# A recorded program, its list scheduler and pinned engine orders in a two-layer hybrid backbone

## The chip, the cores and the metric

One NeuronCore of a Trainium2 chip runs the whole program in one launch. The metric is the device time of an execution in microseconds (us). A difference counts as one only from about 1% on.

## The reference, cut to what matters

Two layers work on 512 latent tokens and 256 context tokens, 1024 wide, in fp32:

```python
for i in range(DEPTH):
    sh1_l, sc1_l, g1_l, sh2_l, sc2_l, g2_l = adaln(c, ada_w[i], ada_b[i])       # silu(c) @ w + b, six sections
    sh1_c, sc1_c, g1_c, sh2_c, sc2_c, g2_c = adaln(c_ctx, ada_w[i], ada_b[i])
    h_l = rmsnorm(x, norm1_g[i]) * (1.0 + sc1_l) + sh1_l
    h_c = rmsnorm(ctx, norm1_g[i]) * (1.0 + sc1_c) + sh1_c
    p_l, p_c = h_l @ w_in[i], h_c @ w_in[i]      # Hyena | gMLP gating | differential attention
    ...
    x = x + g1_l * mix_out(p_l, att_l, hy_params, sg_params, w_out[i])
    x = x + g2_l * swiglu(rmsnorm(x, norm2_g[i]) * (1.0 + sc2_l) + sh2_l, ffn_w1[i], ffn_w2[i])
    if not last:
        ...                                      # the same for ctx
```

The Hyena part convolves with long filters that a small sine MLP gives; they depend on weights alone.

## The kernel before

Each fp32 product is three matmuls of fp32r halves (`mm3`, L251 to L253: high by high, high by low, low by high). What feeds them is split into halves by `split`: ScalarE (ACT) copies the high half (L232) and VectorE (DVE) subtracts for the low half (L233); for weights the raw tile is FW and the halves lie in RW, for activations F and R. The matmuls write into eight PSUM banks (one tile, `banks`). SBUF is four arenas (F, FW, R, RW), and a buffer's place in them is fixed while the Python code runs, so a later buffer waits for the earlier one's readers.

Four generators are woven by rates that the code states: the latent stream, the context stream, a side task (filters and their spectra, from the long-convolution tables), and the modulation (`ada`). The weaving fixes the order in which instructions are recorded. The framework then takes, at the end of its context, each engine's order from these records and its own estimates of durations; an engine issues in the order that it was given.

The names that the prediction uses: `filters` multiplies position features by two small layers (matmuls at L859), and reduces and takes the sine on DVE and ACT (L863, L818 to L824); the result is stored at L870 as `hid`, and `spectra` reads it back (L885) and multiplies it at L905 and L906. `ada` (matmuls at L400) works in steps: a step loads two tiles of 512 KB (L364) and has eight matmuls of 32 columns by 256, four side by side in four column strips of the array; four steps make a section, and sections 0 and 1 give the first layer's modulation. FW holds six such tiles. `norm` squares on ACT and adds on DVE (L459), takes 1/sqrt by a chain of small DVE instructions (L261 to L267, L283), and scales (L482, L506, L507, L510). `attend` reduces a maximum (L686), scales it (L689), takes the exponential on ACT (L691), combines (L695 to L697) and transposes (L706). DMAs of x, ctx and weights are issued by SyncE (SP), the tables by GpSimd (POOL).

```python
for z in range(2):
    for j in range(4):
        k = 2 * i + z
        nc.tensor.matmul(pa[32 * j:32 * j + 32, :], lhsT=self.cv[:, k, :],
                         rhs=ws[j // 2][:, j % 2, z], start=(k == 0), stop=(k == KT - 1),
                         tile_position=(0, 32 * j))
```

Of the kernel before, what the change touches and what calls it, by code (L numbers as in the profile page):

```python
# [2 lines left out]

# [6 lines left out]
F32 = mybir.dt.float32  # L10
# [3 lines left out]
ALU = mybir.AluOpType  # L14
# [18 lines left out]
CW = 256  # L33
# [5 lines left out]
class Buf:  # L39


    def __init__(self, arena, pos, units, ap):
        self.arena, self.pos, self.units, self.ap = arena, pos, units, ap
# [69 lines left out]
class Stream:  # L113


    def __init__(self, name, T, v, home, away, mine):
# [18 lines left out]
POOL = {"in cm": (0, 1),  # L135
        "in tm": (0, 0),
        "out": (0, 1),
        "rope": (0, 0),
        "parity": (1, 0),
        "product 1": (1, 1),  # L140
        "product 2": (1, 0),
        "mix": (0, 2)}
# [7 lines left out]
class Net:  # L150
# [16 lines left out]
    def woven(self, *tasks):  # L167

        live = [[g, r, 0.0, False] for g, r in tasks]
        phase = self.phase
        while live:
            if self.phase != phase:
                phase = self.phase
                for t in live:
                    t[2] = 0.0
            t = min(live, key=lambda t: t[2])
            before = self.cost
            try:  # L180
                t[3] = next(t[0]) == "wait"
            except StopIteration:
                live.remove(t)
                continue
            t[2] += max(self.cost - before, 1.0) / (self.rates[t[1]] if isinstance(t[1], str) else t[1])
            yield "wait" if all(o[3] for o in live) else None
# [1153 lines left out]
def run(gen):  # L1340
    stuck = 0
    for r in gen:
        stuck = stuck + 1 if r == "wait" else 0
        assert stuck < 1000


def network(ctx, tc, A):
    net = Net(ctx, tc, A)
    woven = net.woven
    kd = {(l, L): tc.dram_tile([P, 2, 2, 2, L // 256, HYW], F32, name=f"kd{l}_{L}")  # L1350
# [124 lines left out]
    def side_task():  # L1475
        yield from fil
        yield from spectra(0, SEQ)
        yield from spectra(0, CTX)
        yield from wait("late")
        yield from spectra(1, SEQ)  # L1480
# [26 lines left out]
    side = side_task()  # L1507
    net.first = []
    gens = {"A": ada, "F": fil, "L": lat_gen, "C": con_gen, "S": side, **{k: loads(k) for k in "XBDK"}}
    for g, n in START:  # L1510
        run(take(gens[g], n))
    run(woven((lat_gen, "lat"), (con_gen, "con"), (side, "side"),
              (ada, "ada")))


def flat(ap):
# [106 lines left out]
```

## Time and profile before

| what | value |
|---|---|
| median of 3 runs | 1918.73 us (1917.03 to 1928.58) |
| the profiled execution | 1918.05 us |
| its span, first to last instruction | 1916.3 us |
| mean granted TensorE clock | 0.963 of 2.4 GHz |
| TensorE (PE) matmuls busy | 1797.2 us, 94% |
| VectorE (DVE) busy | 1079.3 us, 56% |
| ScalarE (ACT) busy | 676.9 us, 35% |

Matmuls are pipelined and their ends are modelled, so a duration of one matmul is longer than its distance to the next; distances are read from starts. The matmuls of L400 are recorded twice each, so a step of eight shows as x16.

### The profile page before, as it was taken

What the parts mean: (1) busy time and instruction counts of PE and PEld (TensorE: products, weight loads), DVE (VectorE), ACT (ScalarE), POOL (GpSimd) and SP (SyncE); (2) the same over time, 40 slices, a digit from 0 to 9 for tenths busy, and PEclk for the clock granted to TensorE, in tenths of its full rate; (3) what the DMA queues carried; (4) which work ended last, traced back from release to release, by engine and by line L of the source; (5) the groups of instructions that cost most, each with busy time, mean ns of one, the idle gap of its engine ahead of it and who ended that gap; (6) DMA issues with size and microseconds to landing.
All of it is one profiled execution on the core that took longest, in us unless ns stands there. A gap on an engine that the chain in (4) does not pass through costs nothing.

```text
span 1916.3 us, 27513 instructions
## 1 busy us (share of the span) xinstructions
PE 1797.2 (94%) x10938; PEld 1532.3 (80%) x10938; DVE 1079.3 (56%) x2243; ACT 676.9 (35%) x1167; POOL 118.0 (6%) x127
## 2 busy tenths in 40 slices
PE   4799898888997999999999999899999999999999
PEld 1478798677776888888888888789988798888887
DVE  5677786876868533332323244779588773333333
ACT  2534434443535321212121222633455452222221
POOL 1100223311001000000000000011000000000000
PEclk9799899799997999999999999899999899999999
DMA  8667644335454434343424135453213222323321
GB/s 274 198 222 237 212 155 133 111 101 162 144 174 137 153 99 136 90 136 110 149 86 146 61 112 174 138 171 124 72 43 111 73 62 64 115 83 102 93 93 65
DMA packets 101819, 245.39 MB, mean 128 GB/s; under 512 B 9748, under 2 KB 21750, under 8 KB 101690
## 3 DMA queue, kind: packets, MB, share of 16 engines
q1 hardware_dynamic: 93450, 221.71, 36.3%
q0 software_dynamic: 8240, 21.92, 3.9%
q8 instruction: 86, 1.41, 0.3%
q14 instruction: 43, 0.35, 0.1%
HBM read 221.18 MB, written 22.41 MB: 127 GB/s over the span
## 4 chain that ended last, share of the span: by engine, by line
PE 72%; DVE 7%; ACT 2%; issue 1%; DMA 1%; POOL 0%; DVEq 0%; ACTq 0%
PE banks L251 23%; PE banks L252 22%; PE banks L253 22%; PE banks L706 1%; PE banks L400 1%; DVE tiny L686 1%; PE banks L279 1%; DMA F<-x_ctx 1%; DVE F L459 1%; DVE RW L233 0%; ACT F L506 0%; ACT F L691 0%; DVE F L1028 0%; DVE F L1189 0%; DVE F L1026 0%
## 5 line engine op out<-in xcount | busy, mean ns | idle before, releaser
L251 PE MATMUL banks<-R,RW 128*128 128x512 f32 (+1 forms) x1984 | 698.3, 353 | 8.1 <-ACT R L507 2.9
L252 PE MATMUL banks<-R,RW 128*128 128x512 f32 (+1 forms) x1984 | 695.2, 351 | 2.6 <-DVE R L510 2.6
L253 PE MATMUL banks<-R,RW 128*128 128x512 f32 (+1 forms) x1984 | 693.4, 350 | 1.7 <-DVE RW L233 1.7
L232 ACT ACTIVATE RW<-FW 128x1024 fp32r<-128x1024 f32 (+2 forms) x240 | 240.3, 1002 | 563.9 <-PE banks L252 427.5
L251 PEld LDWEIGHTS banks<-R,RW 128*128 128x128 f32 x1984 | 379.0, 191 | 66.8 <-issue 5.6
L252 PEld LDWEIGHTS banks<-R,RW 128*128 128x128 f32 x1984 | 378.8, 191 | 51.9 <-DVE R L510 3.9
L253 PEld LDWEIGHTS banks<-R,RW 128*128 128x128 f32 x1984 | 378.1, 191 | 50.1 <-DVE RW L233 2.1
L233 DVE TENSOR_TENSOR RW<-FW,RW 128x1024 fp32r<-128x1024 f32 (+2 forms) x228 | 263.1, 1154 | 243.5 <-ACT RW L232 225.7
L1189 DVE SCALAR_TENSOR_TENSOR F<-banks,mods,F 128x512 f32<-128x512 f32 (+1 forms) x192 | 116.3, 615 | 177.1 <-PE banks L253 150.6
L251 PE MATMUL banks<-R 128*128 128x256 f32 (+3 forms) x584 | 185.0, 336 | 30.7 <-ACT R L1039 12.3
L252 PE MATMUL banks<-RW,R 128*128 128x256 f32 x624 | 178.9, 287 | 2.3 <-DVE RW L233 2.2
L251 PE MATMUL banks<-RW,R 128*128 128x256 f32 x624 | 180.1, 289 | 0.8 <-ACT RW L232 0.7
L253 PE MATMUL banks<-RW,R 128*128 128x256 f32 x624 | 179.0, 287 | 0.0
L252 PE MATMUL banks<-R 128*128 128x256 f32 (+3 forms) x584 | 176.6, 316 | 0.0
L253 PE MATMUL banks<-R 128*128 128x256 f32 (+3 forms) x584 | 175.2, 312 | 1.3 <-DVE R L1041 1.3
L251 PEld LDWEIGHTS banks<-R 128*128 128x128 f32 (+1 forms) x584 | 114.8, 205 | 55.9 <-ACT R L1039 14.6
L1207 DVE TENSOR_TENSOR F<-F,banks 128x256 f32<-128x256 f32 (+1 forms) x71 | 40.0, 565 | 203.8 <-PE banks L253 189.9
L232 ACT ACTIVATE R<-F 128x512 fp32r<-128x512 f32 (+1 forms) x133 | 71.8, 550 | 222.9 <-DVE F L1207 159.8
L252 PEld LDWEIGHTS banks<-R 128*128 128x128 f32 (+1 forms) x584 | 117.5, 205 | 8.8 <-issue 3.0
L252 PEld LDWEIGHTS banks<-RW,R 128*128 128x128 f32 x624 | 120.8, 194 | 4.6 <-DVE RW L233 3.7
L251 PEld LDWEIGHTS banks<-RW,R 128*128 128x128 f32 x624 | 120.8, 194 | 3.7 <-issue 1.0
L253 PEld LDWEIGHTS banks<-RW,R 128*128 128x128 f32 x624 | 120.9, 194 | 0.7 <-issue 0.2
(158 smaller groups left out, 1681.1 us busy)
## 6 DMA issues: line engine op xcount, KB each, us to landing
FW<-in_ffn_w SPq DMA_DIRECT2D x104, 512.0 KB, 3.7
FW<-in_ada_w SPq DMA_DIRECT2D x96, 512.0 KB, 5.3
FW<-in_w_in_tm SPq DMA_DIRECT2D x50, 512.0 KB, 4.7
R<-in_tab POOLq DMA_DIRECT2D x28, 512.0 KB, 5.9
FW<-in_w_in_cm SPq DMA_DIRECT2D x24, 512.0 KB, 4.7
F<-x_ctx SPq DMA_DIRECT2D x36, 256.0 KB, 3.4
FW<-in_ffn_w SPq DMA_DIRECT2D x24, 384.0 KB, 3.1
x_ctx<-F SPq DMA_DIRECT2D x32, 256.0 KB, 2.4
```

Of the source, the lines that this page charges most:

```text
L232: self.nc.scalar.activation(hi, src, AF.Copy)
L233: (lo_eng or self.nc.vector).tensor_tensor(lo, src, hi.bitcast(F32), op=ALU.subtract)
L251: mm(out, lhsT=lh, rhs=rh, start=(i == 0), stop=False)
L252: mm(out, lhsT=lh, rhs=rl, start=False, stop=False)
L253: mm(out, lhsT=ll, rhs=rh, start=False, stop=(i == n - 1))
L279: nc.tensor.matmul(p1[:, t:t + 1], lhsT=sq[:, t * P:(t + 1) * P], rhs=self.ones[:, 0:1], start=True, stop=True)
L400: nc.tensor.matmul(pa[32 * j:32 * j + 32, :], lhsT=self.cv[:, k, :], rhs=ws[j // 2][:, j % 2, z], start=(k == 0), stop=(k == KT - 1), tile ...
L459: nc.vector.tensor_tensor(st.acc[:, cols], st.acc[:, cols], q.ap, op=ALU.add)
L686: nc.vector.tensor_reduce(m, b.ap, axis=AX.X, op=ALU.max)
L706: nc.tensor.transpose(p[:, i, z, :], ws[z][:, (a + i) * P:(a + i + 1) * P], self.ident)
L1189: self.nc.vector.scalar_tensor_tensor(x, p, self.mods[l][:, sec * 8 + k, st.v:st.v + 1], x, op0=ALU.mult, op1=ALU.add)
L1207: nc.vector.tensor_tensor(s.ap, s.ap, u, op=ALU.mult)
```

## The change

The code that records instructions runs as before, but on `Plan`, which notes each call with a duration and a pace instead of issuing it. At the end `needs` finds who waits for whom from the regions that calls read and write, `order` runs a list scheduler, and `issue` issues all calls in its order and ties each instruction to the one before it on its engine, so that the framework can't move it. The scheduler takes, whenever an engine is free, the call that can start with the lowest rank: three quarters by its place in the recorded order, one quarter by the longest chain of work that still hangs on it. `note` joins the eight matmuls of an `ada` step into one entry. No computation, buffer or DMA is changed.

```diff
+class Plan:
...
+    RATE, LINE, HANDOVER, DRAIN, LANDING, WINDOW = 2.4, 258.0, 38.0, 163.0, 1620.0, 3413.0
+    def __init__(self, tc, share=0.75):
...
+    def note(self, e, op, args, kw):
...
+        if op == "dma_start":
+            took, pace = math.prod(out.shape) * 4 / self.LINE, 50.0 if e == self.SP else 560.0
+        elif e == self.PE:
+            if op == "transpose":
+                pace, late, ins = 109.0, [args[1]], [args[2]]
+            else:
+                lhs, rhs = kw["lhsT"], kw["rhs"]
+                n, late, ins = size(rhs), [lhs], [rhs]
+                if rhs.dtype != F32 or lhs.dtype != F32:
+                    pace = max(n / self.RATE + 13.5, 109.0)
+                elif size(lhs) <= 32:
+                    pace = 125.0
+                else:
+                    pace = 2 * max(112.0, n / self.RATE)
+            took = pace + self.DRAIN
...
+        elif e == self.POOL:
+            took = 340 + 2.1 * n if kw.get("op") != ALU.pow else 700 + 180 * n
+            pace = took - 40
+        else:
...
+            took = (n + {"tensor_tensor": 148, "tensor_scalar": 155}.get(op, 205 if op[0] == "s" and n > 64 else 140)) / 0.96
+            pace = took - 82
+        call, glue = (op, args, kw), e == self.PE and n == CW and size(out) == CW and size(late[0]) == 32
+        units = [[u for x in side for u in self.region(x)] for side in (outs, ins, late)]
+        if glue and self.todo and self.todo[-1][2]:
+            last = self.todo[-1]
+            last[1].append(call)
...
+    def order(self):
+        todo, needs = self.todo, self.needs()
+        n = len(todo)
+        rest, behind = [0.0] * n, [[] for _ in todo]
+        for k in range(n - 1, -1, -1):
+            rest[k] += todo[k][3] + (self.LANDING if todo[k][1][0][0] == "dma_start" else 0.0)
+            for j, kind in needs[k].items():
+                rest[j] = max(rest[j], rest[k])
+                behind[j].append((k, kind))
+        top = max(rest)
+        rank = [self.share * k / n - (1 - self.share) * rest[k] / top for k in range(n)]
...
+    def issue(self):
+
+        nosync = mybir.DependencyInfo(mybir.DependencyClass.NoSync, mybir.DependencyReason.DATA)
+        last = [None] * 5
+        for k in self.order():
+            e, calls = self.todo[k][:2]
+            for op, args, kw in calls:
+                ins = getattr(getattr(self.tc.nc, Program.engines[e]), op)(*args, **kw).ins
+                if last[e] is not None:
+                    self.tc.add_manual_dep(ins, last[e], nosync, reason="order")
+                last[e] = ins.name
...
 def network(ctx, tc, A):
+    tc = Plan(tc)
     net = Net(ctx, tc, A)
...
     run(woven((lat_gen, "lat"), (con_gen, "con"), (side, "side"),
               (ada, "ada")))
+    tc.issue()
```

Every instruction of the changed kernel carries the line of the call in `issue` (L1571), so its rows are told apart by their tiles.

The first place is the program's head, on SP, whose queue issues the loads of x, the modulation weights (`in_ada_w`), ctx, and the store of the MLP's result (`hid`). Before:

```order
L421 DMA F<-in_x 128x1024 x4
L364 DMA FW<-in_ada_w 128x2x512 x5
L421 DMA F<-in_ctx 128x512 x4
L364 DMA FW<-in_ada_w 128x2x512 x7
L870 DMA hid<-F 128x768
L885 DMA F<-in_hy_w 64x1024 x2
L885 DMA F<-hid 64x512 x2
L894 DMA F<-in_decay 128x1024
L896 DMA F<-in_hy_bias 1x512
L364 DMA FW<-in_ada_w 128x2x512 x4
```

And now:

```order
L1571 DMA FW<-in_ada_w 128x2x512
L1571 DMA F<-in_x 128x1024
L1571 DMA FW<-in_ada_w 128x2x512 x5
L1571 DMA subs_83<-in_subln_g 128x2
L1571 DMA F<-in_ctx 128x512 x3
L1571 DMA F<-in_hy_w 64x1024 x2
L1571 DMA F<-in_ctx 128x512
L1571 DMA F<-in_decay 128x1024
L1571 DMA hid<-F 128x768
L1571 DMA FW<-in_ada_w 128x2x512 x8
L1571 DMA F<-in_hy_bias 1x512
L1571 DMA F<-hid 64x512 x2
```

Six modulation tiles stand ahead of ctx instead of five, and the next seven behind the store of `hid` instead of ahead of it.

The second place is on PE, where the first spectra (R into banks), the modulation steps (FW) and then the first projections (`R,RW`) meet. Before:

```order
L905 MATMUL banks<-R 128x512
L400 MATMUL banks<-FW,cv_82 32x256 x2
L906 MATMUL banks<-R 128x512
L251 MATMUL banks<-R 128x256 x2
L252 MATMUL banks<-R 128x256
L253 MATMUL banks<-R 128x256
L400 MATMUL banks<-FW,cv_82 32x256 x6
L252 MATMUL banks<-R 128x256
L253 MATMUL banks<-R 128x256
L251 MATMUL banks<-R 128x256 x2
L252 MATMUL banks<-R 128x256
L400 MATMUL banks<-FW,cv_82 32x256 x2
```

And now:

```order
L1571 MATMUL banks<-FW,cv_82 32x256 x8
L1571 MATMUL banks<-R 128x512 x8
L1571 MATMUL banks<-FW,cv_82 32x256 x8
L1571 MATMUL banks<-R 128x256 x21
L1571 MATMUL banks<-ident_85,F 128x128 x2
L1571 MATMUL banks<-R 128x256 x11
L1571 MATMUL banks<-FW,cv_82 32x256 x8
L1571 MATMUL banks<-R,RW 128x512 x18
L1571 MATMUL banks<-RW,R 128x256
L1571 MATMUL banks<-R,RW 128x512 x2
L1571 MATMUL banks<-RW,R 128x256 x2
L1571 MATMUL banks<-R,RW 128x512 x6
```

The steps of eight stand whole, while matmuls of two other accumulations, 512 and 256 wide, now alternate.

The third place is on DVE late in the first layer's attention, where the second norm of the latent stream (L482, L510) runs beside the last heads. Before:

```order
L482 TENSOR_TENSOR F<-F,banks 128x256 x4
L686 TENSOR_REDUCE tiny<-banks 128x1
L510 TENSOR_TENSOR R<-F,R 128x256 x2
L482 TENSOR_TENSOR F<-F,banks 128x256 x2
L510 TENSOR_TENSOR R<-F,R 128x256 x2
L482 TENSOR_TENSOR F<-F,banks 128x256 x2
L510 TENSOR_TENSOR R<-F,R 128x256 x2
L689 TENSOR_SCALAR tiny<-tiny,rq_81 128x1
L285 SCALAR_TENSOR_TENSOR tiny<-sums_80 128x4
L510 TENSOR_TENSOR R<-F,R 128x256 x2
L695 RECIPROCAL tiny<-tiny 128x1
```

And now:

```order
L1571 TENSOR_TENSOR F<-F,banks 128x256 x4
L1571 TENSOR_SCALAR tiny<-tiny,rq_81 128x1
L1571 TENSOR_TENSOR R<-F,R 128x256
L1571 TENSOR_TENSOR F<-F,banks 128x256
L1571 TENSOR_TENSOR R<-F,R 128x256 x2
L1571 TENSOR_TENSOR F<-F,banks 128x256 x2
L1571 TENSOR_TENSOR R<-F,R 128x256
L1571 TENSOR_TENSOR F<-F,banks 128x256
L1571 TENSOR_TENSOR R<-F,R 128x256 x3
L1571 RECIPROCAL tiny<-tiny 128x1
```

The scaling of the maximum (the one TENSOR_SCALAR) stood behind ten instructions of the norm after its maximum, and now stands ahead of ten.

## Rows read from the trace of the kernel before

**Rows 1.** Page, part 1: busy us, share of the span, instructions

```profile
PE 1797.2 (94%) x10938; PEld 1532.3 (80%) x10938; DVE 1079.3 (56%) x2243; ACT 676.9 (35%) x1167; POOL 118.0 (6%) x127
```

**Rows 2.** Stretches by stage: length, busy us of five engines, clock, DMA share, GB/s

```profile
0.00:80.00 80.00, 44.34 (x235) 21.31 (x235) 48.66 (x115) 29.00 (x55) 11.69 (x20) 0.88 0.76 254
80.00:660.00 580.00, 522.62 (x3602) 441.81 (x3600) 426.59 (x1023) 258.91 (x493) 84.73 (x82) 0.93 0.51 161
660.00:1200.00 540.00, 540.00 (x3225) 470.12 (x3224) 185.85 (x264) 115.36 (x168) 3.21 (x6) 1.00 0.38 120
1200.00:1560.00 360.00, 338.51 (x2193) 302.17 (x2192) 282.56 (x655) 175.42 (x312) 18.33 (x19) 0.94 0.33 102
1560.00:1912.00 352.00, 351.77 (x1691) 296.85 (x1690) 135.08 (x190) 98.24 (x140) 0.00 (x0) 1.00 0.28 85
```

**Rows 3.** PE's waits, 80 to 660 us: us in total, times, longest

```profile
PE banks L706 <- DVE F L697: 5.9, 4, 4.0
...
PE banks L251 <- ACT F L691: 3.8, 2, 2.9
...
PE banks L251 <- ACT F L1076: 2.6, 1, 2.6
PE banks L252 <- DVE R L510: 2.6, 2, 2.1
```

**Rows 4.** Stretches of 4 us in the head, columns as in rows 2

```profile
24.00:28.00 4.00, 3.21 (x12) 2.54 (x11) 1.75 (x8) 0.90 (x3) 0.00 (x0) 1.00 0.53 156
28.00:32.00 4.00, 2.50 (x19) 0.75 (x17) 2.80 (x9) 0.62 (x2) 0.00 (x0) 1.00 0.38 87
```

**Rows 5.** SP's DMA issues in the head, in order of time: start, us

```profile
6.84 8.83 SPq L364 DMA_DIRECT2D FW<-in_ada_w  x5
24.82 5.50 SPq L421 DMA_DIRECT2D F<-in_ctx  x4
30.37 8.31 SPq L364 DMA_DIRECT2D FW<-in_ada_w  x7
38.78 0.42 SPq L870 DMA_DIRECT2D hid<-F  x1
```

**Rows 6.** DVE in the head, in order of time: start, us, [idle before]

```profile
29.52 1.08 DVE L863 TENSOR_SCALAR F<-banks,F 128x768 f32<-128x768 f32 x1 [1.15 <-PE banks L859]
```

**Rows 7.** DVE and PE around 587 us, in order of time

```profile
582.93 0.95 DVE L686 TENSOR_REDUCE tiny<-banks 128x1 f32<-128x768 f32 x1
...
587.35 0.20 DVE L689 TENSOR_SCALAR tiny<-tiny,rq 128x1 f32<-128x1 f32 x1
...
591.07 1.33 PE L706 MATMUL banks<-ident,F 128*128 128x128 f32 x5 [4.00 <-DVE F L697]
```

**Rows 8.** PE at two modulation steps, whole and cut, in order of time

```profile
152.02 1.07 PE L400 MATMUL banks<-FW,cv 128*32 128x256 f32 x16
153.02 0.39 PE L251 MATMUL banks<-R 128*128 128x256 f32 x1
...
260.97 1.05 PE L400 MATMUL banks<-FW,cv 128*32 128x256 f32 x10
261.95 0.39 PE L251 MATMUL banks<-R 128*128 128x256 f32 x1
262.27 0.63 PE L400 MATMUL banks<-FW,cv 128*32 128x256 f32 x6
262.83 0.38 PE L252 MATMUL banks<-R 128*128 128x256 f32 x1
263.05 0.28 PE L253 MATMUL banks<-R 128*128 128x256 f32 x1
263.17 0.28 PE L251 MATMUL banks<-R 128*128 128x256 f32 x1
```

**Rows 9.** DVE, one instruction beside GpSimd and without it, in order of time

```profile
288.96 1.77 DVE L1029 TENSOR_TENSOR F<-F 128x512 f32<-128x512 f32 x1 [1.19 <-POOL F L1025]
...
295.95 0.68 DVE L1029 TENSOR_TENSOR F<-F 128x512 f32<-128x512 f32 x1
```

154 lines of the change are left out of this document (added).

## The prediction

> **What bounds the kernel now.** I read the busy times first: PE is at 94% of the span, and the next engine, DVE, at 56% [rows 1]. So an order can pay only where PE does not run, or runs slowly. The stretches by stage say where that is [rows 2]. From 660 to 1200 us and from 1560 to 1912 us (the two FFNs) PE is busy for 540.00 of 540 and 351.77 of 352 us, at a granted clock of 1.00. A permutation of the same matmuls can give nothing there: 892 us of the span are out of reach. The loss lies in the other three stretches. Idle PE: 80 - 44.3 = 35.7 us in the head, 580 - 522.6 = 57.4 us in the first layer, 360 - 338.5 = 21.5 us in the second. To this comes the clock, 0.88, 0.93 and 0.94 there: as full-speed time that is at most 0.12 x 80 = 9.6, 0.07 x 580 = 40.6 and 0.06 x 360 = 21.6 us, at most because some of the low clock falls on idle PE. Together about 186 us, the ceiling of any schedule.
>
> Then I asked what PE waits for. In the first layer the view of waits names some twenty producers in 44 waits, and none holds more than a seventh of the 57 us; four of those that the new order touches are in [rows 3]. They are DVE and ACT, and DVE is busy for 426.6 of 580 us there [rows 2]. So PE mostly waits because its operand is not made yet. Moving matmuls on PE alone helps little; what can help is an earlier place for the producer on DVE, ACT or in a DMA queue.
>
> **The change part by part.** It adds and removes no work. The sum is made against the profiled execution, 1918.05 us (span 1916.3 us and 1.75 us around it), which lies 0.7 us under the median; I apply it to the median.
>
> *Head, DMA queue.* SP issued five modulation tiles by 15.7 us (6.84 + 8.83), then nothing until ctx at 24.82 us, whose buffers were still read; the sixth tile, whose place was free, stood behind that, and the next batch went out at 30.37 us [rows 5]. From 24 to 32 us the DMA engines ran at 0.53 and 0.38 of their time, so 4 x 0.47 + 4 x 0.62 = 4.4 us of them were lost [rows 4], in a stretch where PE waits for these weights. Now the sixth tile goes first. The other seven stand behind the store of `hid`, which was issued at 38.78 us [rows 5]: left at that time, it would hold them 8.4 us longer than 30.37. But the sine MLP moves too: its second pass started on DVE at 29.52 us [rows 6] mixed with the norm's small instructions, and now all of it stands ahead of the norm's 1/sqrt chain, and its feature loads are SP's second and third. I expect `hid` near 30 us. Bounds: a loss of 8.4 us if `hid` stays late; 0 if some other link holds; 9.2 us of gain (24.82 - 15.7) if the whole silence of the queue goes. I take 7: the 4.4, and part of what the whole steps save on PE just before the modulation is complete.
>
> The skill bears on this place. In the rows the DMA engines are half idle for 8 us while a free transfer stands in a queue. The Trainium skill, page "Trainium Kernel Development and Optimization", section "Key Constraints", says that DMAs from all queues run on the same 16 DMA engines, so that spreading them over issuers saves issue time only; by that rule alone an earlier issue buys nothing in a saturated stretch, and this term would be 0. The shares of 0.53 and 0.38 show that this stretch was not saturated, so I keep the 7.
>
> *First layer, producers.* At 582.93 us DVE made a maximum, and the scaling of it, 0.20 us long, came only at 587.35 us, behind the norm; PE waited 4.00 us for what follows [rows 7]. The scaling now stands ahead of the norm's instructions, so some 3 us of the delay go; the norm comes some tenths later. I read the same kind of move, one to eight instructions taken from in front of the awaited one, at the waits in [rows 3]: 5.9 + 3.8 + 2.6 + 2.6 = 14.9 us. Others get one to five instructions put in front. Half of 14.9, 7.5 us, because behind each wait the next link is close; bounds 0 and 14.9.
>
> *Clock.* The 40.6 us of the first layer follow idle time. If 7.5 of 57.4 us of idle go, the same share of the clock's loss is 5 us; bounds 0 and 15.
>
> *Steps of eight.* A whole step takes 1.00 us (152.02 to 153.02); one cut into five and three takes 0.98 + 0.56 = 1.54 us [rows 8]. In the old order 27 of the 48 steps stand whole, in the new one all. 21 x 0.54 = 11.3 us at most; I take 8, because some pieces share a run with the next step, and because part falls into idle time. Cost at the other side: a step now starts only when both its tiles have landed, where four matmuls could go before; up to 1 us each, within the next item.
>
> *Second layer.* Its longest waits are a serial chain of a norm, which no order shortens: 2 us of 21.5.
>
> *New waits.* Pinned places rest on durations that miss some things. Bounded by what the moves put in front elsewhere, 0 to 10 us; I take 3. Of the alternating accumulations I put the cost on PE at nothing: PE loads weights for every matmul anyway (as many loads as matmuls, [rows 1]). In the FFNs what hides a later eviction is the other banks' work; if that cover went, it would show as idle in stretches that now have none.
>
> Sum: 7 + 7.5 + 5 + 8 + 2 - 3 = 26.5 us, so 1918.7 - 26.5 = 1892 us.
>
> **The rivals.**
>
> *Nothing was ready anyway.* For it: the producers are busy chains, and the new order lies close to the old one (on DVE an instruction moves 2.8 places on average). Then only the DMA's 4.4 us and the 8 us of whole steps remain, less 3: 1909 us.
>
> *DVE's durations are not fixed.* L1029 took 0.68 us alone and 1.77 us beside GpSimd [rows 9]; the scheduler knows (512 + 148) / 0.96 = 0.69 us only. GpSimd is busy for 84.7 us in 82 instructions in the first layer [rows 2]; if half of them delay a DVE instruction by 1.1 us, DVE's clockwork is off by 45 us in that stage, and the producers' term and the clock's vanish: 7 + 8 + 2 - 3 = 14, so 1905 us. The Trainium skill, page "SBUF — State Buffer", section "Who interferes with whom", states a rule of this kind: a DVE instruction with two SBUF inputs is blocked for the whole length of a GpSimd instruction that reads SBUF. The trace agrees, with 1.77 against 0.68 us.
>
> *Slower: alternating accumulations hand over late.* Place: first and second layer, where PE's matmuls of two banks now alternate. An accumulation of 24 matmuls, 0.12 us apart [rows 8], takes 2.9 us; alternated with another, the first one's result comes up to 2.9 us later, 1.45 on average, and DVE starts later. It eats the gains of head and steps and the 2 us (17 us) from 12 of the 44 hand-offs on, and makes the kernel 1% slower from 25 on; with 30 it is 43.5 - 17 = 26.5 us slower: 1945 us. Against it: the rank follows the recorded order by three quarters, so an older accumulation is mostly ahead.
>
> *Much faster.* If the scheduler removes a third of the idle in both layers (26 us) and of the clock's loss (21 us), with 9 in the head and 8 for steps, less 3: 61 us, 1858 us. Against it: PE's waits have no common cause.
>
> **How the numbers follow.** Forecast 0.52 (1875 to 1908); nothing ready 0.20; DVE's durations 0.08; slower 0.08; much faster 0.12. Faster by over 1% (under 1899.5 us, about what a measurement can tell from no change): four fifths of the forecast and the much faster case, 0.53. Slower: 0.08. Within 1%: 0.39. The range reaches from 1852 us, past the much faster case, to 1920 us, which takes in the late `hid` (7 turned into -8.4 gives 1908 us) with new waits at their bound, and leaves out the slower rival.
>
> **What would show it.** The FFN stretches stay at PE 100% and as long as before. In the head the DMA share between 24 and 32 us rises above 0.8, and the first G (the scale made from section 1) comes 5 to 10 us before its old time. The waits of L706-like transposes shrink, L400 runs show x16 throughout, and the mean clock rises to about 0.97. I am wrong if the head is not shorter (then `hid` was late), if PE idles in the FFNs (then evictions bunch), or if the first layer's stretch keeps its 57 us of idle with other names on it.

## The result, and the profile after

The changed kernel takes 1939.57 us (median of 6 runs, 1937.53 to 1941.05), the kernel before 1918.25 us (6 runs, 1913.33 to 1928.58): a ratio of 1.0099, interval 1.007 to 1.0128. It is about 1% slower; I had forecast 1892 us, in a range from 1852 to 1920.

Page, part 1, of the changed kernel (against [rows 1]):

```profile
PE 1819.3 (94%) x10938; PEld 1546.1 (80%) x10938; DVE 1085.7 (56%) x2243; ACT 677.8 (35%) x1168; POOL 118.6 (6%) x127
```

The span is 1935.9 us, 19.6 more than before, and its mean clock 0.952 (before 0.963). PE's idle time did not grow: 1935.9 - 1819.3 = 116.6 us against 119.1. What grew is PE's busy time, by 22.1 us, for the same 10938 matmuls. The loss to the clock grew by as much: 0.048 x 1935.9 = 92.9 us of full speed, before 0.037 x 1916.3 = 70.9 (some of it falls on idle PE). So the first thing to read here is that PE doesn't wait longer, it runs slower.

The stretches by stage of the changed kernel, cut where about as many matmuls are done as at the cuts of [rows 2], columns as there:

```profile
0.00:68.00 68.00, 39.81 (x210) 20.46 (x214) 46.34 (x99) 22.38 (x37) 10.14 (x17) 0.76 0.87 302
68.00:270.00 202.00, 181.70 (x1224) 152.63 (x1217) 145.40 (x357) 88.30 (x167) 29.12 (x30) 0.90 0.61 190
270.00:674.00 404.00, 359.62 (x2409) 306.55 (x2408) 293.35 (x685) 178.46 (x348) 57.79 (x55) 0.91 0.43 136
674.00:1218.00 544.00, 544.00 (x3228) 468.45 (x3227) 182.89 (x261) 114.27 (x166) 3.21 (x6) 1.00 0.37 118
1218.00:1580.00 362.00, 342.68 (x2194) 301.23 (x2193) 285.67 (x660) 176.47 (x315) 18.34 (x19) 0.94 0.33 102
1580.00:1935.90 355.90, 351.45 (x1691) 296.83 (x1689) 132.10 (x186) 97.89 (x140) 0.00 (x0) 1.00 0.27 85
```

The first layer of the kernel before, halved at the same place:

```profile
80.00:270.00 190.00, 175.26 (x1239) 148.13 (x1236) 140.77 (x343) 83.19 (x150) 27.14 (x27) 0.94 0.66 212
270.00:660.00 390.00, 347.37 (x2365) 293.68 (x2364) 285.82 (x680) 175.72 (x344) 57.59 (x55) 0.93 0.44 136
```

The head is some 12 us shorter (25 matmuls are still to come), the first layer 26 us longer (202 + 404 against 190 + 390) with clocks of 0.90 and 0.91 where 0.94 and 0.93 stood. The FFN is 4 us longer at 100% busy and full clock, the second layer 2 us. I also compared the start of each matmul with the start of the same one before, in groups of 200: 11.9 us earlier near 110 us, 5 us later near 270, 14 later near 660, 17 at the FFN's end, 20 at the end. So the loss is made in the first layer, after a real gain in the head.

The head, in three views of the changed kernel: stretches of 4 us (against [rows 4]), SP's issues (against [rows 5]), and DVE's making of the first G:

```profile
24.00:28.00 4.00, 4.00 (x38) 1.89 (x34) 1.98 (x6) 0.84 (x1) 0.00 (x0) 1.00 1.08 334
28.00:32.00 4.00, 1.91 (x20) 0.78 (x12) 2.92 (x15) 1.59 (x3) 0.00 (x0) 1.00 1.02 308
```

```profile
6.78 8.08 SPq L1571 DMA_DIRECT2D FW<-in_ada_w  x5
...
26.65 0.33 SPq L1571 DMA_DIRECT2D hid<-F  x1
27.07 11.60 SPq L1571 DMA_DIRECT2D FW<-in_ada_w  x8
```

```profile
65.28 0.18 DVE L1571 SCALAR_TENSOR_TENSOR G<-mods,ng 128x16 f32<-128x16 f32 x1
```

`hid` goes out at 26.65 us in place of 38.78, and the modulation tiles behind it at 27.07; the DMA engines are full where they stood at 0.53 and 0.38 (a packet counts where it starts, so a full stretch can read a little over 1). (All instructions now bear L1571, the line of `issue` that emits them; tiles tell them apart.)

What stands on PE at 173 us, in order of time, in the changed kernel:

```profile
172.81 0.28 PE L1571 MATMUL banks<-R 128*128 128x256 f32 x1
172.93 0.28 PE L1571 MATMUL banks<-RW,R 128*128 128x256 f32 x1
173.05 0.28 PE L1571 MATMUL banks<-R 128*128 128x256 f32 x1
173.17 0.28 PE L1571 MATMUL banks<-RW,R 128*128 128x256 f32 x1
```

Two accumulations, one of activations (R) and one with weights (RW), take turns matmul by matmul. Over the program, neighbouring matmuls change the bank 5465 times, before 1486 times (338 and 318 of them are moves between the four strips of a modulation step). How late that makes a result can be read from the starts of the first and the last matmul of each of the 722 accumulations of three matmuls or more outside the modulation: in the first layer 2.15 us apart on average before, 2.90 now; in the second 2.84 and 4.06. These four start 0.12 us apart, as unbroken ones do [rows 8]. This, I thought, costs nothing. The experiments ask whether it does.

### The profile page after: what moved, and what is told of

Its sections match the earlier page's. It is cut to its first block, busy times and chain, and to the rows that moved or that the text cites. A ratio compares the mean times of both kernels' runs of the same rounds, so it can differ in the third digit from the quotient of the medians.

```text
span 1935.9 us, 27529 instructions
## 1 busy us (share of the span) xinstructions
PE 1819.3 (94%) x10938; PEld 1546.1 (80%) x10938; DVE 1085.7 (56%) x2243; ACT 677.8 (35%) x1168; POOL 118.6 (6%) x127
## 4 chain that ended last, share of the span: by engine, by line
PE 83%; DVE 9%; ACT 3%; DMA 2%; issue 2%; SPq 0%; POOL 0%; DVEq 0%; ACTq 0%; POOLq 0%
PE banks L1571 83%; DVE F L1571 5%; ACT F L1571 2%; DVE tiny L1571 2%; DVE RW L1571 1%; ACT R L1571 1%; DVE R L1571 1%; DMA F<-in_x 1%; ACT RW L1571 1%; DMA F<-in_decay 0%; DMA kd<-F 0%; SPq L1571 0%; DMA FW<-in_w_in_tm 0%; DMA F<-x_ctx 0%; DVE inv L1571 0%
## 5 line engine op out<-in xcount | busy, mean ns | idle before, releaser
L1571 PE MATMUL banks<-R,RW 128*128 128x512 f32 (+1 forms) x5952 | 1163.6, 353 | 10.2 <-DVE F L1571 5.9
L1571 PEld LDWEIGHTS banks<-R,RW 128*128 128x128 f32 x5952 | 969.7, 191 | 169.0 <-issue 9.4
L1571 ACT ACTIVATE RW<-FW 128x1024 fp32r<-128x1024 f32 (+2 forms) x240 | 240.3, 1002 | 626.2 <-PE banks L1571 543.7
L1571 DVE TENSOR_TENSOR RW<-FW,RW 128x1024 fp32r<-128x1024 f32 (+2 forms) x228 | 264.9, 1163 | 302.1 <-ACT RW L1571 289.6
L1571 PE MATMUL banks<-R 128*128 128x256 f32 (+4 forms) x1792 | 348.1, 339 | 38.1 <-ACT R L1571 14.3
L1571 PEld LDWEIGHTS banks<-R 128*128 128x128 f32 (+1 forms) x1792 | 275.1, 212 | 93.8 <-issue 27.9
L1571 PE MATMUL banks<-RW,R 128*128 128x256 f32 x1872 | 267.8, 290 | 16.9 <-DVE RW L1571 10.1
L1571 PEld LDWEIGHTS banks<-RW,R 128*128 128x128 f32 x1872 | 245.9, 195 | 26.0 <-DVE RW L1571 12.1
L1571 DVE SCALAR_TENSOR_TENSOR F<-banks,mods,F 128x256 f32<-128x256 f32 (+1 forms) x192 | 116.2, 615 | 152.3 <-PE banks L1571 132.0
L1571 DVE TENSOR_TENSOR F<-F,banks 128x256 f32<-128x256 f32 (+1 forms) x169 | 81.9, 510 | 193.2 <-PE banks L1571 167.4
L1571 ACT ACTIVATE R<-F 128x512 fp32r<-128x512 f32 (+2 forms) x235 | 119.1, 527 | 165.0 <-DVE F L1571 131.4
L1571 ACT ACTIVATE F<-banks 128x512 f32<-128x512 f32 (+1 forms) x196 | 93.8, 491 | 221.6 <-PE banks L1571 194.6
L1571 DVE TENSOR_TENSOR R<-F,R 128x512 fp32r<-128x512 f32 (+2 forms) x227 | 127.3, 576 | 51.3 <-ACT R L1571 50.5
L1571 DVE TENSOR_TENSOR F<-F 128x256 f32<-128x256 f32 (+1 forms) x188 | 117.8, 646 | 8.8 <-ACT F L1571 6.8
L1571 ACT ACTIVATE F<-banks,tiny,rq 128x768 f32<-128x768 f32 (+1 forms) x80 | 72.1, 903 | 64.2 <-DVE tiny L1571 53.9
L1571 PE MATMUL banks<-ident,F 128*128 128x128 f32 x360 | 70.4, 309 | 19.4 <-DVE F L1571 10.8
L1571 ACT ACTIVATE R<-banks 128x512 fp32r<-128x512 f32 (+1 forms) x114 | 54.1, 508 | 74.2 <-PE banks L1571 70.3
L1571 DVE TENSOR_REDUCE tiny<-banks 128x1 f32<-128x768 f32 (+1 forms) x80 | 67.0, 846 | 21.9 <-PE banks L1571 21.9
L1571 DVE TENSOR_TENSOR R<-banks,R 128x512 fp32r<-128x512 f32 (+1 forms) x114 | 63.2, 578 | 23.0 <-ACT R L1571 22.5
L1571 PEld LDWEIGHTS banks<-ident,F 128*128 128x128 f32 x360 | 47.4, 156 | 34.7 <-DVE F L1571 14.8
L1571 PE MATMUL banks<-FW,cv 128*32 128x256 f32 x768 | 61.7, 443 | 4.4 <-DMA FW<-in_ada_w 4.4
L1571 POOL TENSOR_TENSOR F<-F 128x256 f32<-128x256 f32 (+1 forms) x40 | 47.8, 1200 | 206.5 <-DVE F L1571 172.4
```

The lines of the kernel that those rows point to most:

```text
L1571: ins = getattr(getattr(self.tc.nc, Program.engines[e]), op)(*args, **kw).ins
```

## The experiments

Each is the changed kernel with the edit shown, timed with the kernel before on the same chip. The kernel before took 1917.02, 1915.62, 1921.22 and 1916.32 us (medians) in the four groups: 1 to 4, 5 to 8, 9 to 12, 13 to 16. That is 5.6 us from lowest to highest, so runs of different groups are best compared by their distance from it ("over before", of medians); the changed kernel itself lies 21.3 us over.

| | edit | bank changes | median us | over before, us | ratio to before, interval |
|---|---|---|---|---|---|
| e1 | PE stays with its accumulation | 1361 | 1930.31 | 13.3 | 1.0055, 1.0025 to 1.0084 |
| e2 | share 1.0 | 1473 | 1944.35 | 27.3 | 1.0114, 1.0072 to 1.0156 |
| e3 | no unit of eight | 5518 | 2014.11 | 97.1 | 1.0475, 1.043 to 1.0519 |
| e4 | new order in the head alone | 1528 | 1914.24 | -2.8 | 0.9983, 0.9956 to 1.0009 |
| e5 | each unit of eight twice | - | 1969.31 | 53.7 | 1.0273, 1.0243 to 1.0303 |
| e6 | e1 up to 440 us | 1459 | 1916.05 | 0.4 | 0.9997, 0.9968 to 1.0027 |
| e7 | alternate always | 9478 | 2047.25 | 131.6 | 1.067, 1.0628 to 1.0713 |
| e8 | delay beside GpSimd known | 5560 | 1931.10 | 15.5 | 1.0077, 1.0048 to 1.0106 |
| e9 | e1 and e8 | 1389 | 1932.49 | 11.3 | 1.0058, 1.0039 to 1.0078 |
| e10 | e1 and e8 up to 590 us | 1442 | 1923.24 | 2.0 | 1.0002, 0.9977 to 1.0026 |
| e11 | rank by accumulation | 1569 | 1914.46 | -6.8 | 0.9973, 0.9951 to 0.9994 |
| e12 | e11 and e8 | 1571 | 1925.59 | 4.4 | 1.0028, 1.0007 to 1.005 |
| e13 | share 0.70 | 5986 | 1940.45 | 24.1 | 1.0113, 1.007 to 1.0155 |
| e14 | share 0.80 | 5000 | 1941.18 | 24.9 | 1.0103, 1.005 to 1.0157 |
| e15 | e11, share 0.70 | 1619 | 1921.88 | 5.6 | 1.0017, 0.9996 to 1.0038 |
| e16 | e11, share 0.80 | 1549 | 1919.70 | 3.4 | 1.0011, 0.9991 to 1.0031 |

**e1, PE stays.** `more[k]` is the next matmul of k's accumulation:

```diff
-            k = heapq.heappop(can[e])[1]
+            go = more.get(last) if e == self.PE else None
+            if go is not None and not left[go] and at[go] <= now and go not in gone:
+                k = go
+            else:
...
```

> The new order with one rule more: PE goes on with the accumulation it has begun as long as that one's next matmul can start, so neighbouring matmuls change the bank 1361 times and not 5465 (before: 1486). Theory A (alternating accumulations cost the time: each is finished later, its consumer on DVE or ACT starts later, and a matmul behind one of another bank starts a nanosecond or more later): the first FFN gets its 4 us back, the first layer most of the 26 us it lost, so 1910 to 1917 us. Theory B (the quarter of the rank that counts the longest chain puts work in the wrong place): the switches go, but not the loss, 1932 to 1940 us. Theory C (the clock's low stretches fall by chance, and any new order moves them): anywhere from 1915 to 1940 us, with the low-clock time alone deciding.

Measured 1930.31 us: 8 of the 21 us come back, so neither A nor B as I had put them. C's range has it, but the low clock did not decide: the traced clock is 0.949, under the 0.952 of the changed kernel. The starts of the same matmuls say where: near 650 us the order is 2 us ahead of the kernel before and not 14 behind, and the FFN has its 4 us again; but some 12 us are lost between 1447 and 1526 us, where PE's waits end with attention's exponential.

**e2, share 1.0.** `def __init__(self, tc, share=1.0)`.

> The new order with the rank by the recorded place alone (share 1.0); 1473 bank switches, an instruction of PE stands 5.5 places from the old order on average (after: 10.6). Theory A and theory B both expect the loss gone here and the head's gain kept: 1905 to 1918 us. What tells them apart is the run above: A has both kernels equal, B has this one 15 us or more below it. Theory C: 1915 to 1940 us.

Measured 1944.35 us, above every expectation, theory A's too. The quarter for the longest chain is no fault: without it, and without alternation, the order is worse still. Theory B has fallen. But A does not explain this run either. Its trace has the loss in the first layer, where accumulations stay open hardly longer than before: near 110 us its matmuls are 9.7 us earlier than in the kernel before, near 660 us 21.3 later, with PE idle for 77 of 613 us there (57 of 580 before) and a clock of 0.89 (0.93). So an order can lose as much without alternating, and why this one does stays open.

**e3, no unit of eight.** `call, glue = (op, args, kw), False`.

> The new order without the unit of eight: every modulation matmul is scheduled by itself. My prediction's term: 21 steps more are cut, 0.54 us each, up to 11.3 us slower than the new order, 1945 to 1951 us. Rival: the cut pieces lie beside idle time or cost nothing, since the array takes as many weight loads either way: 1936 to 1942 us. A gain of the unit below 3 us would say that I mis-sized that term.

Measured 2014.11 us, 74 us slower than the new order, far above my upper value. The modulation's group of instructions on PE (busy us, mean ns, idle before), in the changed kernel and then in e3:

```profile
L1571 PE MATMUL banks<-FW,cv 128*32 128x256 f32 x768 | 61.7, 443 | 4.4 <-DMA FW<-in_ada_w 4.4
```

```profile
L1571 PE MATMUL banks<-FW,cv 128*32 128x256 f32 x768 | 139.1, 422 | 13.5 <-DMA FW<-in_ada_w 13.5
```

Left to itself the scheduler puts them one or two at a time between others (102 runs of one matmul, 39 of two), and scattered so the same matmuls keep PE busy for more than twice as long. The first FFN alone, always busy, becomes 46 us longer than in the new order.

**e4, the head alone.**

What the scheduler starts before 100 us is issued in its order and pinned, the rest as recorded and not pinned.

```diff
+            if now < 100.0e3:
+                head.append(k)
...
+        return head, [k for k in range(n) if k not in done]
...
-                if last[e] is not None:
+                if last[e] is not None and k in pin:
```

> The new order only for what the scheduler starts in its first 100 us; everything behind it is issued in the recorded order and left to the framework (1528 bank switches, PE 0.9 places from the old order on average). If the head's gain of 8 to 12 us that the trace of the new order shows is real and lasts: 1906 to 1911 us, faster than both. If what the head gains is only borrowed (later loads come no earlier, PE waits for them instead): 1916 to 1920 us. If the loss between 100 and 270 us comes from the head itself (buffers and queues left in a worse state), 1925 to 1935 us.

Measured 1914.24 us, 2.8 below the kernel before and level with it by the interval. In its profile the matmuls near 110 us start 12.8 us earlier than before, those near 210 us only 5.4, and from there nothing is lost any more. The head's gain is real, but 7 of its 12 us are borrowed: at 186.57 us PE waits 2.52 us for what a load of `decay` releases, and that load lands 5.5 us earlier than before, not 12.

**e5, each unit twice.**

```diff
+            if self.todo[k][2]:
+                calls = [(op, args, {**kw, "stop": False}) for op, args, kw in calls] + [(op, args, {**kw, "start": False}) for op, args, kw in calls]
```

> The new order with each of the 47 modulation units issued twice in a row (the second copy adds to the same accumulation, so the modulation comes out doubled; nothing else differs): about 1.05 us of PE work more for each, 13 of them in the first FFN, 25 in the first layer, 9 in the head. Theory D (in the layers PE waits for chains of other engines, so that PE work saved or added there turns into idle time and low clock, and not into time; only in the FFNs PE work is time): 1940 + 13.5 + at most 8, so 1953 to 1961 us, with less low-clock time in the first layer. If PE work is time everywhere: 1940 + 13.5 + 26, and some of the head's, so 1979 to 1990 us.

Measured 1969.31 us, between the two. 47 x 1.05 = 49 us of work became 30 us of time: 11 in the FFN, 16 to 20 in the first layer, few in the head. Theory D is wrong as stated: in the first layer 0.6 to 0.8 us of time came for each unit of 1.05.

**e6, e1 up to 440 us.** As e4, with e1's rule and 440 in place of 100.

> The order that stays with an accumulation, pinned for what the scheduler starts in its first 440 us (near 470 us in the trace of that kernel, where it led the kernel before by 9 to 10 us); everything behind it is issued in the recorded order and left to the framework. If places before 470 us decide what was gained there and the rest goes as in the kernel before: 1905 to 1910 us, faster than both. If the lead is given back by a rest that fits less well: 1914 to 1920 us. If any pinned stretch costs clock somewhere: above 1920 us.

Measured 1916.05 us, with a wide spread (1906.47 to 1927.26). The profiled execution was the fastest of ten and kept a lead of 9.9 us over the kernel before through the first FFN; the median keeps none.

**e7, alternate always.**

```diff
             k = heapq.heappop(can[e])[1]
+            if e == self.PE:
+                if k == more.get(last) and can[e]:
+                    other = heapq.heappop(can[e])[1]
+                    heapq.heappush(can[e], (rank[k], k))
+                    k = other
+                last = k
```

> The suspected cost doubled: the new order, but PE takes another accumulation's matmul after each one if one can start; 9478 changes of bank between neighbours (the new order: 5465). Theory A, as far as it is PE's own pace (new order against the one that stays with an accumulation: 18 us of work for 4100 changes, 4.4 ns each): 18 us more, 1953 to 1963 us, and the first FFN, which has no idle, longer by some 5 us or more. If alternation costs nothing by itself: 1935 to 1944 us.

Measured 2047.25 us: 108 us slower than the new order, six times what I had expected of PE's pace. The first FFN, with 3104 changes against 2081, is only 1.2 us longer (1.2 ns a change). The price lies in the layers: in the profiled execution 65 us in the first and 47 in the second. Accumulations stay open 4.11 us there (2.90 in the new order) and 5.68 us (4.06). But that is not all that differs there. In the FFNs the matmuls have 128 rows; in the layers some have 64, and now those of 64 and of 128 take turns, at the full clock:

```profile
179.15 0.39 PE L1585 MATMUL banks<-RW,R 128*128 128x256 f32 x1
179.47 0.38 PE L1585 MATMUL banks<-R 64*128 64x256 f32 x1
179.78 0.38 PE L1585 MATMUL banks<-RW,R 128*128 128x256 f32 x1
180.09 0.38 PE L1585 MATMUL banks<-R 64*128 64x256 f32 x1
```

They start 0.31 us apart, where matmuls of 128 rows that alternate start 0.12 apart.

**e8, the delay beside GpSimd.** `apart`: no input in a bank.

```diff
+            if e == self.DVE and free[self.POOL] - 40 > now and todo[k][1][0][0] == "tensor_tensor" and apart(k):
+                wait = min(free[self.POOL] - 40 - now, 1083)
+                took, pace = took + wait, pace + wait
```

> The new order by a scheduler that knows one thing more: a tensor_tensor of DVE with both inputs in SBUF takes longer by the rest of a GpSimd instruction that runs when it starts, up to 1.08 us (1.77 against 0.68 us in the trace of before). My rival 'DVE's durations are not fixed': the 7 us that the trace of the new order loses between 246 and 262 us, where DVE is late by such instructions and PE waits 5.61 us, come back: 1928 to 1934 us. If that loss has another reason: 1936 to 1944 us.

Measured 1931.10 us, in the range of my rival. The place it was meant for, in the changed kernel, first DVE and GpSimd, then PE, in order of time:

```profile
248.78 3.50 DVE L1571 TENSOR_TENSOR F<-F 128x512 f32<-128x512 f32 x2
...
248.94 2.79 POOL L1571 TENSOR_TENSOR RW<-FW,RW 128x1024 fp32r<-128x1024 f32 x1
```

```profile
255.08 0.55 PE L1571 MATMUL banks<-RW,R 128*128 128x256 f32 x1 [5.61 <-DVE F L1571]
```

Two instructions that the scheduler takes for 0.69 us each take 3.50 together, and PE waits 5.61 us. But in e8 the stretch from 180 to 270 us (of before) stayed about as long; of what came back (8 us by the medians, 6 over before) the trace has some 6 us between 270 and 400 us. So the time agreed and the place did not.

**e9 and e10, both rules.**

> Two rules that each gave back a part, together: PE stays with its accumulation (alone 9 us faster than the new order) and the scheduler knows the delay of DVE beside GpSimd (alone 8 us faster). If they mend different losses: 1939.6 - 9 - 8, so 1919 to 1925 us. If both mend the same one: 1928 to 1932 us.

> Both rules, pinned for what the scheduler starts in its first 590 us (the head and the first layer), the rest in the recorded order and left to the framework. Theory: the first layer then keeps a lead of about 10 us over the kernel before, and FFN and second layer go as before: 1905 to 1911 us. Against it the order pinned to 440 us, whose lead in its profile was 10 us and whose median was level with the kernel before: then 1913 to 1918 us.

Measured 1932.49 and 1923.24 us. The rules do not add: e9 is level with e1 (11.3 and 13.3 us over before). And pinning the first layer only (e10) gives no lead; both expectations for it were too low.

**e11, rank by accumulation.**

```diff
+        head = {}
+        for k, t in enumerate(todo):
+            if t[0] == self.PE and t[1][0][0] == "matmul":
+                key = tuple(sorted(set(t[6])))
+                if t[1][0][2]["start"]:
+                    head[key] = rank[k]
+                rank[k] = head[key]
```

> The new order, but all matmuls of an accumulation take the rank of its first one: PE goes on with the older accumulation and still turns at once to one that ranks ahead (1569 bank changes; the order that stays: 1361). If alternation is the loss in the first layer, and the 13 us that the order that stays lost in the second layer come from finishing a long accumulation while a short urgent one waits: 1917 to 1924 us. If alternation is not what cost the time, and staying helped by chance: 1932 to 1942 us.

Measured 1914.46 us, 25 below the new order (28 over before) and, by its interval, 0.1 to 0.5% faster than the kernel before: the fastest of the kernels run here in relation to it, though within what I called no change. The same place on PE in its trace, in order of time:

```profile
170.33 3.04 PE L1578 MATMUL banks<-RW,R 128*128 128x256 f32 x24
173.21 0.60 PE L1578 MATMUL banks<-ident,F 128*128 128x128 f32 x4
173.56 1.68 PE L1578 MATMUL banks<-R 128*128 128x256 f32 x12
```

24 matmuls of one accumulation, then 12 of another. And the loss of e1 in the second layer is gone (what the kernel before does between 1380 and 1560 us takes about 179 us, in e1 about 192).

**e12, e11 with e8's rule.**

> The rank by accumulation, and the scheduler that knows the delay of DVE beside GpSimd. If the two effects add and the second layer keeps its time: 1908 to 1916 us, level with or faster than the kernel before. If the new order loses something in every form: 1920 to 1932 us.

Measured 1925.59 us, 11 slower than e11. The rule that gave 6 to 8 us to one order takes 11 from another: orders that differ a little scatter by such amounts. Then the 25 us of e11 could be scatter too.

**e13 to e16, the same pair at two other shares.** `share=0.7` and `share=0.8`, without and with e11's rule.

> The new order with share 0.70 in place of 0.75 (alternating as the new order does, 5986 bank changes). Theory A: alternation is the loss, whatever the exact order: 1933 to 1948 us. Theory C (orders scatter by some 10 us each way, and the 25 us between the new order and the rank by accumulation are two draws): as likely below 1928 us as above.

> The new order with share 0.80 (5000 bank changes). Theory A: 1930 to 1945 us. Theory C: as likely below 1928 us as above.

> The rank by accumulation with share 0.70 (1619 bank changes). Theory A: 10 us or more below the alternating order of the same share, and 1910 to 1928 us. Theory C: no difference between the two families of orders.

> The rank by accumulation with share 0.80 (1549 bank changes). Theory A: 10 us or more below the alternating order of the same share, and 1910 to 1928 us. Theory C: no difference between the two families.

Measured 1940.45 and 1941.18 us alternating, 1921.88 and 1919.70 by accumulation. The three alternating orders lie within 2 us of each other, and each is 18 us or more above its partner: 25.1, 18.6 and 21.5 us. That isn't scatter: at these three shares alternation is what costs. e8, the one alternating order that did better, still lies 5.5 us above its partner e12 (11 over before). Theory A's wider claim, that an order without alternation loses nothing, has e2 against it.

## Why the prediction was wrong, point by point

**The step that failed** is "Of the alternating accumulations I put the cost on PE at nothing". In the three pairs alternation costs 25.1, 18.6 and 21.5 us, as much as the whole loss of the change (21); with e8's rule in both orders it costs 5.5 to 11. I had the mechanism among the rivals, "alternating accumulations hand over late", at 1945 us, and gave it 0.08, because the rank follows the recorded order by three quarters. What I overlooked in the code: each matmul of an accumulation ranks a little behind the one before it. An accumulation that is recorded later, but hangs on a longer chain, begins first, and as soon as its next matmul ranks level with the other's, the two take turns.

It is not the whole miss. Without alternation (e11, e15, e16) the kernel is level with the one before, and not 26.5 us faster: the terms for the first layer's producers and the clock failed too (below). And the rival's 1945 us came near the measured time with only part of the mechanism, so in part by luck.

How the 22 us (the mean of the three pairs) are made up I worked out from the traces: for every matmul the distance to the next start, less the gap between them, sorted by the granted clock; time at the low level counts half as work. On average alternation adds 10.7 us of work, 9.0 us for time at the low level, and 2.2 us of idle PE (single executions; over all runs the mean clocks of a pair differ by 0.001 to 0.004, 2 to 8 us).

The work is not the price of changing the bank. In the changed kernel's trace, neighbours of 256 columns and equal rows start 0.12 us apart at the full clock (median), with a change of bank (1103 pairs) and without (3167), and its first FFN has 1780 more changes than that of e11 and 0.5 us more work. It is the price of changing between 64 and 128 rows: 0.31 us where 0.12 would do in the rows of e7, 0.21 (median of 40 pairs of 256 columns at the full clock) in the changed kernel. Such neighbours number 235, 249 and 230 in the alternating orders and 185, 176 and 182 in their partners, and what they take beyond 0.12 us each differs by 9.6, 14.5 and 10.3 us: that is all of the work, and other pairs of neighbours even out. In e7 they number 455, and 49 us lie there, again all of the 48 us of work that e7 adds to the new order; 47 more are low clock and 19 idle PE. That these come from late results fits the longer open accumulations, but no run separates it from PE's slower pace, and how either becomes time at the low clock the runs do not show.

**Head, 7 us: right in its links.** `hid` at 26.65 us (I expected about 30), the DMA engines full, no silence over 1.2 us in SP's queue before it. The gain is 12 us at 110 us, but 5 to 7 last (e4); "part of what the whole steps save" stood in this term and in the steps' own. The first G comes 2.7 us earlier, not 5 to 10. The shares of 1.08 and 1.02 where 0.53 and 0.38 stood confirm that there was room. The Trainium skill, page "Trainium Kernel Development and Optimization", section "Key Constraints", states that DMAs from all queues run on the same 16 DMA engines; by it an earlier issue would buy nothing where these are full, and here they were not.

**Steps of eight, 8 us: about right.** The group's busy time fell from 71.5 to 61.7 us. Counted as above, the neighbours into and out of the strips take 11.4 us less work than before (130 pairs became 92), near the 11.3 that I had as the most. With e5's rate of 30 us for 49 of work that is worth some 7 (an estimate). The changes between 64 and 128 rows, 10.6 us more than before, take it back. Without the unit the scheduler loses 74 us (e3).

**First-layer producers, 7.5 us: nothing came.** PE's waits, 68 to 674 us, in the changed kernel (against [rows 3]; us in total, times, longest):

```profile
PE banks L1571 <- DVE F L1571: 27.2, 13, 5.6
PE banks L1571 <- ACT R L1571: 12.1, 8, 4.0
PE banks L1571 <- ACT F L1571: 10.9, 8, 2.9
```

Idle PE is 20.3 + 44.4 = 64.7 us there, where it was 57.4. The place that I had read closely shows why (against [rows 7]), DVE and PE in order of time:

```profile
593.34 0.95 DVE L1571 TENSOR_REDUCE tiny<-banks 128x1 f32<-128x768 f32 x1
...
596.04 0.21 DVE L1571 TENSOR_SCALAR tiny<-tiny,rq 128x1 f32<-128x1 f32 x1
...
603.21 1.02 DVE L1571 SCALAR_TENSOR_TENSOR F<-F,tiny 128x768 f32<-128x768 f32 x1
...
604.29 1.54 PE L1571 MATMUL banks<-ident,F 128*128 128x128 f32 x6 [3.48 <-DVE F L1571]
```

From maximum to scaling it is 1.75 us now and was 3.47, so the move did what it says. PE waits 3.48 us for the transposes behind it, and waited 4.00: half a microsecond is left of the 3 that I counted. I had read DVE and PE there and not ACT, which takes the exponential next. In the kernel before:

```profile
587.84 0.71 ACT L507 ACTIVATE R<-F 128x256 fp32r<-128x256 f32 x2
588.45 0.97 ACT L691 ACTIVATE F<-banks,tiny,rq 128x768 f32<-128x768 f32 x1
```

And in the changed kernel:

```profile
596.37 1.09 ACT L1571 ACTIVATE F<-F,mods,G 128x256 f32<-128x256 f32 x2
...
601.15 0.60 ACT L1571 ACTIVATE F<-F,mods,G 128x256 f32<-128x256 f32 x1
601.65 0.98 ACT L1571 ACTIVATE F<-banks,tiny,rq 128x768 f32<-128x768 f32 x1
```

The exponential started when ACT was done with the norm, so an earlier scaling alone could give nothing; and now 13 instructions of the norm stand between the scaling and it on ACT, so that from maximum to exponential it is 7.36 us, and was 4.57.

**Clock, +5 us: it went the other way,** by 22 us over the program (0.963 to 0.952). I had tied the clock to idle time. The first layer's idle time grew by 7.3 us, which by the prediction's own share costs 5; its loss to the clock grew from 40.6 to 0.10 x 202 + 0.09 x 404 = 56.6 us. Alternation is a part of that. But the orders by accumulation stand at 0.950 to 0.954 in their traces too. They have the head's gain and 9 to 11 us less work than the kernel before, and end level with it: counted as above, the low level costs them 15 to 21 us more (over all runs their mean clocks are 0.953 to 0.956, those of the kernel before 0.960 and 0.961, which is 8 to 16 us). What in the scheduler's orders holds the clock down stays open.

**DVE's durations (rival, 1905 us).** The mechanism is in the trace (3.50 us for two, beside a GpSimd instruction of 2.79). The Trainium skill, page "SBUF — State Buffer", section "Who interferes with whom", states that a DVE instruction with two SBUF inputs contends with a GpSimd instruction that reads SBUF; the trace agrees. But letting the scheduler know of it gave 6 to 8 us once (e8), nothing to speak of once (e9), and -11 once (e12): not what decides here.

**Second layer and FFNs.** Idle went from 21.5 to 19.3 us in the second layer, as forecast, and yet it is 2 us longer. The FFNs stay at 100%; I had said no time could change there, and 3.6 us did. e1 has them back; with e11 not, so alternation is not shown to be their cause.

## What to carry to other kernels

A list scheduler that ranks single matmuls should rank accumulations: a result counts when its last matmul is done, two accumulations that share PE fairly both come late, and where their matmuls differ in rows every turn costs PE itself; here that is some 20 us of 1940. Put such operations as belong together on the machine into one unit before anything is ordered. Follow a shortened wait through every engine up to PE: one more queue can eat the gain. And when several orders are tried, repeat a comparison at another setting before believing it: single orders without alternation lay some 30 us apart here (e2 and e11), and only the repeated pairs told the cause.

## What the runs showed of the hardware that I had not expected

Matmuls of two banks can take turns for nothing (0.12 us apart, at 173 us of the changed kernel), but matmuls of 64 and of 128 rows cannot (0.31 us apart, at 179 us of e7).

A busy PE can stay at the low clock. The same 15 us of the program's time in the kernel before and then in the changed one, columns as in rows 2:

```profile
190.00:205.00 15.00, 12.57 (x87) 8.78 (x86) 9.13 (x24) 5.43 (x13) 3.44 (x4) 0.89 0.71 218
```

```profile
190.00:205.00 15.00, 13.71 (x48) 8.90 (x50) 10.74 (x29) 6.84 (x18) 3.24 (x5) 0.50 0.60 198
```

In the changed kernel PE had waited 2.36 us at 186.75; from 189.1 us on it ran at 1.2 GHz for 27.3 us, although it was busy for 13.71 of these 15 us, and did 48 matmuls where the kernel before did 87 (not the same ones). In e7 PE shows as busy without a gap and the clock is still at the low level, or back at it:

```profile
1480.00:1490.00 10.00, 10.00 (x32) 7.00 (x32) 5.39 (x10) 3.12 (x5) 0.00 (x0) 0.65 0.00 0
1510.00:1520.00 10.00, 10.00 (x31) 7.26 (x31) 4.49 (x11) 2.80 (x6) 0.00 (x0) 0.50 0.01 2
```

Busy here does not mean dense: 31 or 32 matmuls in 10 us are more than 0.3 us apart. In these stretches the share of busy PE did not tell the level; the profile's clock column has to be read beside it.
